# A weight's block sums computed in an earlier stage and passed through DRAM, in a decoder block on one core

## The chip, the core and the metric

The kernel runs on one NeuronCore of a Trainium2 chip. The metric is the time of one execution in microseconds of device time. Several executions give a median. The profile is that of one further execution. It shows five engines: PE (matrix products; PEld loads its weights), DVE (vector), ACT (activations), POOL, and SP, which here only issues DMA transfers. Each engine works through its own list of instructions in order. Transfers issued by SP are one queue, those issued by POOL another, and both move over the core's 16 DMA engines.

## The reference

One decoder block for 1024 tokens of width 1024, all in float32. What matters here, with the attentions left out:

```python
def reference(x, mem, ...):
    h = rmsnorm(x, g_mix_norm[l])
    proj = jnp.einsum('bsd,de->bse', h, w_in[l])
    # q, k, v of two attentions, memory queries, gate logits
    ...
    gates = jax.nn.sigmoid(gate_logit.reshape(b, s, N_BRANCH, D_MODEL))
    merged = gates[:, :, 0] * br_sb + gates[:, :, 1] * br_fox + gates[:, :, 2] * br_mem
    x = x + jnp.einsum('bsd,de->bse', merged, w_out[l])

    h2 = rmsnorm(x, g_mlp_norm[l])
    u = jax.nn.relu(jnp.einsum('bsd,df->bsf', h2, w_ff_up[l]))
    return x + jnp.einsum('bsf,fd->bsd', u * u, w_ff_down[l])
```

`w_out` is 1024x1024, 4 MB.

## The kernel before

**Arithmetic.** A float32 product is made of three passes: each operand is split into a high part (ACT copies it to the matrix engine's type) and a low part (DVE subtracts the high part from the operand), and PE adds high times high, high times low and low times high. The large products are cut into 2x2 blocks of 512 and made with seven block products instead of eight, named P1 to P7, of sums and differences of blocks. For the output projection the right operand is `w_out`, with blocks W11, W12, W21, W22 (the first figure counts the rows). The right sides that aren't a plain block are W12 - W11 (called `wr12` below), `raw2` = W22 - wr12, and the two differences W21 - raw2 and raw2 - W11.

**Stages.** In order of time: norm of the input; projections (to about 500 us); two attentions and the memory attention; three gated branches added up (`merged`, held in tiles `acc`); the output projection with the residual and the second norm (about 957 to 1058 us); the two products of the MLP.

**Output projection.** The order of its products is `OUT = ("P1", "P2", "P6", "P5", "P3", "P7", "P4")`. A product has four tiles of 128 tokens by 512 columns; a tile is 12 matmuls of 128x512 on PE (L2234). `right_side` splits the right operands (`rounded`: a copy on ACT, a subtraction on DVE), `left_side` the left ones. `residual` adds each finished tile to the rows of `x`, which are loaded into tiles `xm` (shown as `h`), on DVE; after a row block's last tile, its square on ACT gives the row sums, `normed` makes the reciprocal root on small tiles (DVE, ACT) and scales the row (half on ACT, L2291; half on DVE, L2293), and `turn_half` transposes it on PE (L2316, four 128x128 pieces at a time) for the MLP. All plain element-wise operations of this part on DVE stand at L1928, the helper `tt`.

**What sets the order.** The program is written as generators that `spawn` starts. An in-kernel planner (`Machine`) runs them against a model of the engines with a cost for each operation (`dve_time`, `act_time`) and a rate for transfers, and issues every instruction in the order in which the model starts it. `spawn(..., late)` sets how urgent a generator is: a larger figure stands back. One run of the planner covers projections, attentions and two branches, a second one the output projection and the first products of the MLP. The third branch, `last_branch`, lies between the two and is ordered in the usual way of the framework. So an instruction added in one place can move others.

**The weight before.** `last_branch` loads the four blocks of `w_out` into the tiles `wr["11"]`, `wr["12"]`, `wr["22"]`, `wr["21"]` (1 MB each, SP). DVE makes wr12 = W12 - W11 there (one 128x2048 subtraction) and at its end `raw2` (four of 128x512). After the split of P6's right operand, `right_side` makes the other two differences in place (eight of 128x512) and then fires `sums_made`, on which `left_side` waits.

In the projections the tiles of the pool `RAW` (`ra` and `rb`, 128x1024) hold weights on their way to sums and splits; `value_steps` and the gate projections store their results to `v_sb` and `gate_scr` through SP.

Of the kernel before, what the change touches and what calls it, by code (L numbers as in the profile page):

```python
# [14 lines left out]
F32 = mybir.dt.float32  # L15
# [3 lines left out]
ALU = mybir.AluOpType  # L19
AX = mybir.AxisListType  # L20

P = 128
# [21 lines left out]
def tile_hybrid_block(  # L44
# [20 lines left out]
    nc = tc.nc  # L65
# [20 lines left out]
    dram = ctx.enter_context(tc.tile_pool(name="dram", bufs=1, space=bass.MemoryType.DRAM))  # L86
# [35 lines left out]
    v_scr = {k: dram.tile([P, ST * 512], F32, name=f"v_{k}", tag=f"v_{k}") for k in ("sb0", "sb1", "fx0", "fx1")}  # L122
    vr_scr = dram.tile([S + 1, 512], F32, name="vr_scr", tag="vr_scr")
    m_scr = [dram.tile([P, 4, 512], F32, name=f"m_scr{c}", tag=f"m_scr{c}") for c in range(2)]
    x2_scr = dram.tile([S, D], F32, name="x2_scr", tag="x2_scr")
    u_scr = dram.tile([P, S // 2], F32, name="u_scr", tag="u_scr")
    s_scr = dram.tile([7 * DFF // 2, S // 2], F32, name="s_scr", tag="s_scr")
# [56 lines left out]
    class Machine:  # L184
# [12 lines left out]
        def spawn(self, gen, late=0.0):  # L197

            done = Event()
            proc = [gen, late, done, None]  # L200
            self.at(self.now, lambda: self.resume(proc, None))
            return done
# [82 lines left out]
    spawn = machine.spawn  # L285
# [7 lines left out]
    def dve_time(*cols):  # L293
        return sum(0.08 + 0.00105 * m for m in cols)

    def transfer(fn, size, issue=0.1, rate=250e3, queue_="SP"):

        yield Op(queue_, issue, fn, 0.0)
        machine.pipe = max(machine.now, machine.pipe) + size / rate
        yield Sleep(machine.pipe + 2.0 - machine.now)  # L300
# [64 lines left out]
    WP, RAW = Places(list(zip(made_w["whi"], made_w["wlo"]))), Places(made_w["raw"])  # L365
# [1002 lines left out]
    prepped, p_ops, landed_ = ({(u, kind): Event() for u in PROJ for kind in KINDS} for _ in range(3))  # L1368
# [160 lines left out]
    def unit_final(u, ct, q, src, of_bank=False):  # L1529
# [29 lines left out]
        else:  # L1559
# [8 lines left out]
                                      t_.rearrange("p (h n) -> p h n", h=2))  # L1568
            yield from counted(u, c, spawn(normed_turned(src, ss, hd, {"mq": gmq, "fxk": gk2, "fxq": gq2}[u], out_), 1.0))

    def masked(t):
        nc.gpsimd.memset(t, 0.0)
        nc.gpsimd.affine_select(out=t[:, 384:], in_=t[:, 384:], pattern=[[-1, P + 1]], compare_op=ALU.is_ge,
                                fill=-NEG, base=0, channel_multiplier=1)
# [10 lines left out]
    def value_steps():  # L1585

        t = yield Get(SN)
        yield Op("DVE", SMALL, lambda: nc.vector.memset(t[0:1, :], 0.0))
        yield from stored(lambda: nc.sync.dma_start(vr_scr[0:1, :], t[0:1, :]), t)
        for c in range(2):  # L1590
            yield in_scr["sbv", c]
            yield Sleep(1.0)
            evs = []
            for g in range(4):
                three = yield Get(SN, 3)

                def issue():
                    for r0, t in zip((1 + g * 256, g * 256), three):
                        nc.sync.dma_start(t.rearrange("p (i n) -> p i n", i=2),
                                          vr_scr[r0:r0 + 256, c * 256:(c + 1) * 256].rearrange("(i p) n -> p i n", p=P))  # L1600
                yield from transfer(issue, P * 4096, 0.2)
                evs.append(spawn(value_step(c, g, *three)))
            for ev in evs:
                yield ev
            machine.fire(stepped[c])
# [239 lines left out]
    with tc.manual_schedule():  # L1845
        spawn(prologue())
        spawn(unit_loads())
        spawn(unit_prep(), -4.0)
        spawn(forget(), 5.0)
        spawn(value_steps(), 0.0)  # L1850
        spawn(second_part())
        spawn(more_banks())
        spawn(load_pairs(), -20.0)
        spawn(memory(), -300.0)
        spawn(after_kv(kv_tasks))
        spawn(all_h([t.done for t in h_tasks]))
        spawn(loader(tasks))
        spawn(operands(), 100.0)
        spawn(units(True))
        spawn(units(False))  # L1860
        spawn(dense(), 3.0)
        machine.run()
        assert all(pair.over.fired for pair in pairs) and "ws" in holder
# [18 lines left out]
    def last_branch(gpool, os_, ws):  # L1882
        b = order[2][0]
        for d2 in range(4):
            w = ws[d2] if d2 < len(ws) else load_w([(0, w_br[b][:, d2 * 256:(d2 + 1) * 256])], 4, 256)
            if d2 == 3:
                hi, lo = right_tiles("P1")
                for q in range(2):
                    raw = wr["11"][:, 2 * q:2 * q + 2]
                    nc.scalar.activation(hi[q], raw, AF.Copy)  # L1890
                    tt(lo[q], raw, f32(hi[q]), ALU.subtract)
            for dd in range(2):
                d = 2 * d2 + dd
                gt = gpool.t("gt", [P, S])
                nc.sync.dma_start(gt, gate_scr[b * D + d * P:b * D + (d + 1) * P, :])
                if d in (1, 2, 3, 4):
                    key = ("11", "12", "22", "21")[d - 1]
                    k_, n_ = int(key[0]) - 1, int(key[1]) - 1
                    nc.sync.dma_start(wr[key], w_out[k_ * 512:(k_ + 1) * 512, n_ * 512:(n_ + 1) * 512].rearrange(
                        "(k p) n -> p k n", p=P))  # L1900
                nc.scalar.activation(gt, gt, AF.Sigmoid)
                if d == 7:
                    nc.scalar.activation(C.t("st", [P, 8])[:, :1], gt[:, :1], AF.Sqrt, bias=one, scale=0.0)
                for half in range(2):
                    cols = slice(half * 512, half * 512 + 512)
                    ps = mmbank()
                    mm3(ps, [((w[0][:, k, dd * P:(dd + 1) * P], w[1][:, k, dd * P:(dd + 1) * P]), os_[k][half])
                             for k in ks])
                    a_, tm = acc[d][:, cols], gpool.t("tmp", [P, 512])
                    tt(tm, ps, gt[:, cols], ALU.mult)  # L1910
                    tt(a_, a_, tm, ALU.add)
                    if half == 0:
                        hi, lo = left["P1" if d < 4 else "P2"][d % 4]
                        nc.scalar.activation(hi, a_, AF.Copy)
                        tt(lo, a_, f32(hi), ALU.subtract)
                if d == 5:
                    tt(wr["12"], wr["12"], wr["11"], ALU.subtract)
                if d >= 4:
                    k = d - 4
                    a11, a21, a22 = acc[k][:, :512], acc[k][:, 512:], acc[d][:, 512:]  # L1920
                    tt(raw1[k], a21, a22, ALU.add)
                    tt(a21, a11, a21, ALU.subtract)
                    tt(a11, raw1[k], a11, ALU.subtract)
        for k in range(4):
            tt(raw2[k], wr["22"][:, k], wr["12"][:, k], ALU.subtract)

    def tt(out_, a_, b_, op):
        nc.vector.tensor_tensor(out_, a_, b_, op)  # L1928
# [10 lines left out]
    wr = {key: RB.t("h", [P, 4, 512]) for key in ("12", "22", "11", "21")}  # L1939
# [18 lines left out]
    for s in range(0, ST, 2):  # L1958
        t = RA.t("h", [P, 2, D])
# [93 lines left out]
    with tc.manual_schedule():  # L2053
# [81 lines left out]
        def rounded(hi, lo, raw, n):  # L2135
            yield Op("ACT", act_time(n), lambda: nc.scalar.activation(hi, raw, AF.Copy))
            yield Op("DVE", dve_time(n), lambda: tt(lo, raw, f32(hi), ALU.subtract))

        def each(late, *gens):
            for ev in [spawn(g, late + 0.2 * i) for i, g in enumerate(gens)]:  # L2140
                yield ev

        def right_side():

            src = {"P2": "21", "P5": "12", "P3": "22", "P7": "11", "P4": "21"}
            for kind in OUT[1:]:
                n = OUT.index(kind)
                if n >= 2:
                    yield out_issued[OUT[n - 2]]
                hi, lo = right_tiles(kind)  # L2150
                if kind == "P6":
                    yield from each(0.0, *(rounded(right[kind][0][k], right[kind][1][k], raw2[k], 512) for k in range(4)))
                else:
                    raw = wr[src[kind]]
                    yield from each(0.0, *(rounded(hi[q], lo[q], raw[:, 2 * q:2 * q + 2], 1024) for q in range(2)))
                machine.fire(right_made[kind])
                if kind == "P6":
                    for key in ("21", "11"):
                        for k in range(4):
                            a_, b_ = (wr[key][:, k], raw2[k])[::1 if key == "21" else -1]  # L2160
                            yield Op("DVE", dve_time(512), lambda: tt(wr[key][:, k], a_, b_, ALU.subtract))
                    machine.fire(sums_made)

        def left_side():
# [570 lines left out]
```

## Time and profile before

| | |
|---|---|
| time, median of 3 runs | 1667.91 us (1666.76 to 1668.11) |
| the profiled execution | 1668.89 us |
| its span | 1667.1 us |
| mean granted PE clock | 0.999 |
| busy: PE, PEld, DVE, ACT, POOL | 1654.5, 1434.6, 1292.5, 848.9, 256.3 us |
| instructions of PE, DVE, ACT, POOL | 9118, 2079, 1474, 440 |
| DMA read and written | 189.83 MB and 92.83 MB |

The span runs from the first to the last instruction of the profiled execution; the time of that execution contains 1.8 us more. A timeline row gives the start in us from the span's beginning, the duration in us, engine, line, operation, result<-operands, the shape and a count; in square brackets stands how long the engine was idle before the row and what it waited for. `SPq` is SP's issue of transfers. A row of windows gives the window, its length, and for PE, PEld, DVE, ACT and POOL the busy time with the number of instructions in it, then the granted PE clock, the busy share of the DMA engines, and GB/s. [...]

### The profile page before, as it was taken

How to read it: one execution, taken by the hardware profiler on the slowest of the kernel's cores; microseconds unless marked ns; L12 is line 12 of the kernel's file. 1: busy time of each engine (PE TensorE's matmuls, PEld its weight loads, DVE VectorE, ACT ScalarE, POOL GpSimd, SP SyncE). 2: the span in 40 equal slices, each digit the busy share in tenths (PEclk: the TensorE clock that was granted, in tenths of full speed). 3: DMA queues.
4: the chain of work that ended last, by engine and by line, in shares of the span. 5: the costliest groups of instructions: out<-in, count | busy, mean ns of one | idle time of the engine just before them, and what ended most of it. 6: DMA issues, size and time to landing. Idle time of an engine off the chain costs nothing.

```text
span 1667.1 us, 24994 instructions
## 1 busy us (share of the span) xinstructions
PE 1654.5 (99%) x9118; PEld 1434.6 (86%) x9118; DVE 1292.5 (78%) x2079; ACT 848.9 (51%) x1474; POOL 256.3 (15%) x440
## 2 busy tenths in 40 slices
PE   9999999999999999999999999999999999999999
PEld 9998899998888888888888887878888888888887
DVE  7978778855459889868878798987777776787875
ACT  6445555535458898877761446533333345333331
POOL 0001000000153142245400011011122120000000
PEclk9999999999999999999999999999999999999999
DMA  7445534468474455577747643144444475564532
GB/s 247 149 161 170 165 114 137 141 182 255 140 237 145 147 160 162 140 222 222 244 142 215 219 168 104 58 158 150 148 158 158 151 275 211 181 213 169 202 126 76
DMA packets 142222, 284.32 MB, mean 171 GB/s; under 512 B 16914, under 2 KB 53330, under 8 KB 142099
## 3 DMA queue, kind: packets, MB, share of 16 engines
q1 hardware_dynamic: 110562, 183.08, 32.5%
q0 software_dynamic: 31536, 99.64, 19.9%
q8 instruction: 72, 1.18, 0.3%
q14 instruction: 52, 0.42, 0.1%
HBM read 189.83 MB, written 92.83 MB: 170 GB/s over the span
## 4 chain that ended last, share of the span: by engine, by line
PE 72%; issue 14%; DVE 7%; POOL 3%; DMA 3%; ACT 1%; SPq 0%; POOLq 0%; ACTq 0%; DVEq 0%
PE pp L1466 11%; PE pp L1154 10%; PE sc L1466 7%; PE pp L2672 7%; PE sc L1154 6%; PE tr L927 4%; PE tr L2672 4%; PE sc L2672 4%; POOL s_scr L2009 3%; PE pv L1466 3%; PE pv L2672 2%; PE sc L944 2%; PE pp L944 2%; DVE h L1928 2%; DVE tmp L1928 1%
## 5 line engine op out<-in xcount | busy, mean ns | idle before, releaser
L1992 PE MATMUL pp<-h,oh 128*128 128x512 f32 x384 | 118.7, 390 | 1.2 <-ACT cu L2077 0.9
L934 DVE TENSOR_TENSOR ptl<-tr,pth 128x512 fp32r<-128x512 f32 (+1 forms) x160 | 99.0, 628 | 23.9 <-ACT pth L932 23.1
L932 ACT ACTIVATE pth<-tr 128x512 fp32r<-128x512 f32 (+1 forms) x160 | 87.4, 557 | 33.5 <-PE sc L944 14.6
L1992 PEld LDWEIGHTS pp<-h,oh 128*128 128x128 f32 x384 | 71.9, 188 | 17.2 <-ACT cu L2077 1.7
L1383 POOL DMA_DIRECT2D raw<-w_in x32 | 24.2, 757 | 394.8 <-DVE la L1065 207.6
L1992 PE MATMUL pp<-h,ol 128*128 128x512 f32 x192 | 74.9, 390 | 0.0
L853 DVE TENSOR_TENSOR_SCAN e<-r,e 128x384 f32<-128x384 f32 (+3 forms) x64 | 66.3, 1044 | 6.8 <-ACT e L838 6.4
L2672 PE MATMUL pp<-h,h 128*128 128x512 f32 x288 | 66.6, 389 | 0.0
L2672 PE MATMUL pp<-sop,sop 128*128 128x512 f32 x288 | 66.6, 389 | 0.0
L2672 PEld LDWEIGHTS pp<-sop,sop 128*128 128x128 f32 x288 | 54.1, 188 | 11.2
L2672 PEld LDWEIGHTS pp<-h,h 128*128 128x128 f32 x288 | 54.1, 188 | 11.2
L927 PE MATMUL tr<-ident,e 128*128 128x128 f32 x416 | 62.5, 272 | 0.0
L927 PEld LDWEIGHTS tr<-ident,e 128*128 128x128 f32 x416 | 50.5, 140 | 9.9 <-DVE ptl L934 0.2
L2009 POOL DMA_DIRECT2D s_scr<-cu x48 | 26.1, 544 | 191.7 <-DVE cu L1999 183.6
L1014 POOL DMA_DIRECT2D h<-sbk_scr x64 | 33.3, 526 | 95.5 <-PE pv L151 29.5
L944 PE MATMUL sc<-pth,v 128*128 128x256 f32 (+1 forms) x170 | 47.4, 301 | 0.0
L2587 ACT ACTIVATE h<-t 128x2048 fp32r<-128x2048 f32 (+1 forms) x9 | 15.4, 1725 | 60.2 <-DVE t L1928 56.1
L1154 PE MATMUL sc<-h,hc 128*128 128x512 f32 (+1 forms) x154 | 44.8, 375 | 0.0
L1928 DVE TENSOR_TENSOR x<-x,pp 128x512 f32<-128x512 f32 x39 | 26.6, 682 | 22.8 <-PE pp L2672 22.8
L1065 DVE TENSOR_TENSOR lb<-raw,hb 128x1024 fp32r<-128x1024 f32 x20 | 24.5, 1223 | 25.6 <-ACT hb L1064 25.5
L2009 POOL DMA_DIRECT2D s_scr<-s x60 | 32.5, 542 | 71.4 <-DVE s L1928 64.8
L1992 PEld LDWEIGHTS pp<-h,ol 128*128 128x128 f32 x192 | 36.0, 188 | 8.1 <-DVE ol L1928 0.6
(792 smaller groups left out, 5540.3 us busy)
## 6 DMA issues: line engine op xcount, KB each, us to landing
ur<-s_scr SPq DMA_DIRECT2D x26, 1024.0 KB
raw<-w_in POOLq DMA_DIRECT2D x32, 512.0 KB, 4.8
raw<-w_up SPq DMA_DIRECT2D x60, 256.0 KB
s_scr<-s POOLq DMA_DIRECT2D x60, 256.0 KB, 2.7
g<-w_down SPq DMA_DIRECT2D x14, 1024.0 KB
s_scr<-cu POOLq DMA_DIRECT2D x48, 256.0 KB, 2.9
h<-sbk_scr POOLq DMA_DIRECT2D x64, 128.0 KB, 3.1
o<-gate_scr SPq DMA_DIRECT2D x32, 256.0 KB
```

The lines of the kernel that those rows point to most:

```text
L853: nc.vector.tensor_tensor_scan(out=back, data0=rho[:, :u][:, ::-1], data1=back, initial=0.0 if last else beta[:, c + u:c + u + 1], op0=ALU ...
L927: nc.tensor.transpose(tr[:, jj * 256 + a * P:jj * 256 + (a + 1) * P], es[a][:, j * P:(j + 1) * P], ident)
L932: yield Op("ACT", act_time(512 - lo_c), lambda: nc.scalar.activation(ph[:, lo_c:], tr[:, lo_c:], AF.Copy))
L934: yield Op("DVE", dve_time(512 - lo_c), lambda: nc.vector.tensor_tensor(pl[:, lo_c:], tr[:, lo_c:], f32(ph[:, lo_c:]), ALU.subtract))
L944: nc.tensor.matmul(pv[0][:, c_:256], pair.v[:, j, b, :], p_[:, jj * 256 + c_:(jj + 1) * 256], start=(k == 0 and n_ == 0 and i == 0), stop= ...
L1014: nc.gpsimd.dma_start(f32(t[k][rows_, :]), src)
L1154: nc.tensor.matmul(ps, a_, b_, start=(first and i == 0), stop=(last and i == n - 1))
L1466: nc.tensor.matmul(out_, a_, b_, start=(first and n == 0 and j == 0), stop=(last and n == 3 and j == len(todo) - 1), skip_group_check=True)
L1928: nc.vector.tensor_tensor(out_, a_, b_, op)
L1992: nc.tensor.matmul(ps, w[a_][:, k * P:(k + 1) * P], h[b_][k], start=(first and k == 0 and i == 0), stop=(last and k == 3 and i == 2), skip ...
L2009: nc.gpsimd.dma_start(s_scr[r0:r0 + P, :], t)
L2672: nc.tensor.matmul(ps, a_[:, c, qs], b_[:, c, :], start=(kind in ("P1", "P2", "P7") and c == 0 and i == 0), stop=(kind in ("P2", "P4", "P3 ...
```

## The change

A new generator `out_sums` makes all four differences in the projections. It starts once the first right operand of one of the gate projections is prepared, and works through `w_out` in four bands of 128 rows per block: take two `RAW` tiles, load four 128x512 pieces (256 KB each, SP), four DVE subtractions, store the four results (256 KB each, SP) to a DRAM tile `wo_scr`, give the tiles back. That is 32 transfers and 16 DVE instructions. A next band's loads into the same tiles come after the stores that read them.

`last_branch` then loads W11, W21 and W22 from `w_out` and the ready difference for `wr["12"]` from DRAM, fetches `raw2` as four transfers after the sixth gate block, and replaces `wr["11"]` by its ready difference with a transfer of 1 MB at its end. `right_side` starts a transfer of 1 MB into `wr["21"]` after P2's split, and P4's split waits for it. The 13 DVE subtractions there are gone.

```diff
+    wo_scr = {key: dram.tile([P, 4, 512], F32, name=f"wo_{key}", tag=f"wo_{key}") for key in ("11", "12", "21", "22")}
...
+    def out_sums():
+
+        yield prepped["ga", "P1"]
+        for k in range(4):
+            got = yield Get(RAW, 2)
+            t11, t12, t21, t22 = (t[:, i * 512:(i + 1) * 512] for t in got for i in range(2))
+
+            def issue():
+                for t, key in ((t11, "11"), (t12, "12"), (t22, "22"), (t21, "21")):
+                    r0, c0 = (int(key[0]) - 1) * 512 + k * P, (int(key[1]) - 1) * 512
+                    nc.sync.dma_start(t, w_out[r0:r0 + P, c0:c0 + 512])
+            yield from transfer(issue, 4 * P * 2048, 0.4)
+            for out_, a_, b_ in ((t12, t12, t11), (t22, t22, t12), (t21, t21, t22), (t11, t22, t11)):
+                yield Op("DVE", dve_time(512), lambda: nc.vector.tensor_tensor(out_, a_, b_, ALU.subtract))
+
+            def store():
+                for t, key in ((t12, "12"), (t22, "22"), (t21, "21"), (t11, "11")):
+                    nc.sync.dma_start(wo_scr[key][:, k, :], t)
+            yield Op("SP", 0.4, store, 3.0)
+            RAW.put(*got)
...
         spawn(value_steps(), 0.0)
+        spawn(out_sums(), 8.0)
...
                 if d in (1, 2, 3, 4):
-                    key = ("11", "12", "22", "21")[d - 1]
+                    key = ("11", "21", "12", "22")[d - 1]
...
-                    nc.sync.dma_start(wr[key], w_out[k_ * 512:(k_ + 1) * 512, n_ * 512:(n_ + 1) * 512].rearrange(
-                        "(k p) n -> p k n", p=P))
+                    nc.sync.dma_start(wr[key], wo_scr["12"] if key == "12" else w_out[
+                        k_ * 512:(k_ + 1) * 512, n_ * 512:(n_ + 1) * 512].rearrange("(k p) n -> p k n", p=P))
...
                 if d == 5:
-                    tt(wr["12"], wr["12"], wr["11"], ALU.subtract)
+                    for k in range(4):
+                        nc.sync.dma_start(raw2[k], wo_scr["22"][:, k, :])
...
-        for k in range(4):
-            tt(raw2[k], wr["22"][:, k], wr["12"][:, k], ALU.subtract)
+        nc.sync.dma_start(wr["11"], wo_scr["11"])
...
                     raw = wr[src[kind]]
+                    if kind == "P4":
+                        yield in21
...
+                if kind == "P2":
+                    in21 = spawn(transfer(lambda: nc.sync.dma_start(wr["21"], wo_scr["21"]), 4 * P * 2048))
                 if kind == "P6":
-                    for key in ("21", "11"):
-                        for k in range(4):
-                            a_, b_ = (wr[key][:, k], raw2[k])[::1 if key == "21" else -1]
-                            yield Op("DVE", dve_time(512), lambda: tt(wr[key][:, k], a_, b_, ALU.subtract))
                     machine.fire(sums_made)
```

The order of instructions changes on DVE and SP in the projections, and on DVE, ACT, SP and PE in the output projection. The rows below give the line, the operation, result<-operands with a number for each buffer, and the shape. Lines of the changed kernel are 1 to 23 higher, and buffer numbers are shifted.

DVE in the projections, from 361.45 to 367.31 us of the profile before; L1396 makes weight sums, L1513 adds product tiles, L1065 splits:

```order
L1396 TENSOR_TENSOR s_155<-raw_153,raw_154 128x1024
L1513 TENSOR_TENSOR sn_149<-sn_149,pv_140 128x512
L1396 TENSOR_TENSOR raw_153<-raw_151,raw_153 128x1024
L1396 TENSOR_TENSOR raw_151<-s_155,raw_151 128x1024
L1513 TENSOR_TENSOR sn_147<-sn_147,pp_135 128x512
L1396 TENSOR_TENSOR raw_152<-raw_152,raw_151 128x1024
L1065 TENSOR_TENSOR la_165<-raw_151,ha_163 128x1024
```

The same stretch with the change; L1585 is `out_sums`:

```order
L1397 TENSOR_TENSOR s_159<-raw_157,raw_158 128x1024
L1514 TENSOR_TENSOR sn_153<-sn_153,pv_144 128x512
L1397 TENSOR_TENSOR raw_157<-raw_155,raw_157 128x1024
L1585 TENSOR_TENSOR ra_168<-ra_168 128x512
L1397 TENSOR_TENSOR raw_155<-s_159,raw_155 128x1024
L1514 TENSOR_TENSOR sn_151<-sn_151,pp_139 128x512
L1397 TENSOR_TENSOR raw_156<-raw_156,raw_155 128x1024
L1585 TENSOR_TENSOR rb_170<-rb_170,ra_168 128x512
L1585 TENSOR_TENSOR rb_170<-rb_170 128x512
L1066 TENSOR_TENSOR la_169<-raw_155,ha_167 128x1024
L1585 TENSOR_TENSOR ra_168<-rb_170,ra_168 128x512
```

Four of the new subtractions stand between the weight's sums and splits that PE waits for.

DVE at the end of the third branch and the start of the output projection, before; `raw_9281` to `raw_9284` are `raw2`, `rb` is the low part of P2's right operand, and the rows on `g_7467` and `raw_9288` make left sums:

```order
L1928 TENSOR_TENSOR lb_9658<-h_9264,hb_9656 128x1024
L1928 TENSOR_TENSOR raw_9288<-g_7467,g_7469 128x512
L1928 TENSOR_TENSOR raw_9281<-h_9262,h_9261 128x512
L1928 TENSOR_TENSOR g_7467<-g_7467 128x512
L1928 TENSOR_TENSOR raw_9282<-h_9262,h_9261 128x512
L1928 TENSOR_TENSOR g_7467<-raw_9288,g_7467 128x512
L1928 TENSOR_TENSOR raw_9283<-h_9262,h_9261 128x512
L1928 TENSOR_TENSOR raw_9284<-h_9262,h_9261 128x512
L1928 TENSOR_TENSOR ol_9664<-g_7466,oh_9660 128x512
L1928 TENSOR_TENSOR rb_9659<-h_9264,ra_9657 128x1024
```

And with the change:

```order
L1951 TENSOR_TENSOR lb_9710<-h_9316,hb_9708 128x1024
L1951 TENSOR_TENSOR raw_9340<-g_7519,g_7521 128x512
L1951 TENSOR_TENSOR ol_9716<-g_7518,oh_9712 128x512
L1951 TENSOR_TENSOR g_7519<-g_7519 128x512
L1951 TENSOR_TENSOR rb_9711<-h_9316,ra_9709 128x1024
L1951 TENSOR_TENSOR g_7519<-raw_9340,g_7519 128x512
L1951 TENSOR_TENSOR h_9684<-h_9684,pp_9700 128x512
```

The four `raw2` rows are gone, one left split (`ol`) stands earlier, and `rb` comes after one left sum fewer.

PE in the output projection where P3 has ended (`pv` is its last tile) and P7 begins (`sc`), before; L2316 are the turns of the rows in `h`:

```order
L2234 MATMUL pv_9655<-ha_9904,ol_9896 128x512
L2234 MATMUL sc_9651<-hb_10013,cu_9931 128x512
L2234 MATMUL sc_9651<-lb_10015,cu_9931 128x512
L2234 MATMUL sc_9651<-hb_10013,cu_9935 128x512
L2316 MATMUL pp_9648<-ident,h_9632 128x128 x4
L2316 MATMUL pp_9649<-ident,h_9632 128x128 x4
L2234 MATMUL sc_9651<-hb_10013,cu_9932 128x512
L2234 MATMUL sc_9651<-lb_10015,cu_9932 128x512
L2234 MATMUL sc_9651<-hb_10013,cu_9936 128x512
L2316 MATMUL pp_9650<-ident,h_9632 128x128 x4
```

And with the change, where L2339 are the turns:

```order
L2257 MATMUL pv_9707<-ha_9970,ol_9889 128x512
L2339 MATMUL pp_9700<-ident,h_9684 128x128 x4
L2339 MATMUL pp_9701<-ident,h_9684 128x128 x4
L2339 MATMUL pp_9702<-ident,h_9684 128x128 x4
L2257 MATMUL sc_9703<-hb_10060,cu_9937 128x512
L2257 MATMUL sc_9703<-lb_10062,cu_9937 128x512
L2257 MATMUL sc_9703<-hb_10060,cu_9941 128x512
```

Three turns stand straight after P3's last matmul, ahead of all of P7; before, three matmuls of P7 stood ahead of the first two turns and three more ahead of the third.

## Prediction

> **What bounds the kernel now.** I read the engine line of the page first, then what the tensor engine (PE) waits for, then its granted clock and its rows around the longest wait, and last the vector engine (DVE) there.
>
> ```profile
> span 1667.1 us, 24994 instructions
> PE 1654.5 (99%) x9118; PEld 1434.6 (86%) x9118; DVE 1292.5 (78%) x2079; ACT 848.9 (51%) x1474; POOL 256.3 (15%) x440
> ```
>
> PE is busy for 1654.5 of 1667.1 us, and its instructions stay as many. So the change can only give back PE's waits and slow stretches, or add some. The waits of PE, in total, times and longest:
>
> ```profile
> PE pp L2316 <- ACT h L2291: 3.0, 1, 3.0
> ...
> PE pp L1992 <- ACT cu L2077: 0.9, 2, 0.7
> ...
> PE sc L2234 <- DVE rb L1928: 0.6, 1, 0.6
> ```
>
> The first and the last lie in the output projection, where the removed work stands. PE there, and DVE's and ScalarE's (ACT's) part of the chain that PE waits for:
>
> ```profile
> 973.68 0.39 PE L2234 MATMUL sc<-ra,cu 128*128 128x512 f32 x1
> 974.63 0.50 PE L2234 MATMUL sc<-rb,cu 128*128 128x512 f32 x1 [0.56 <-DVE rb L1928]
> ...
> 1011.04 0.39 PE L2234 MATMUL pp<-ha,ol 128*128 128x512 f32 x1
> ...
> 1016.49 0.39 PE L2234 MATMUL pv<-ha,ol 128*128 128x512 f32 x1
> 1016.71 0.39 PE L2234 MATMUL sc<-hb,cu 128*128 128x512 f32 x1
> ...
> 1017.16 0.39 PE L2234 MATMUL sc<-hb,cu 128*128 128x512 f32 x1
> 1020.51 1.63 PE L2316 MATMUL pp<-ident,h 128*128 128x128 f32 x8 [2.95 <-ACT h L2291]
> ```
> ```profile
> 1016.37 0.67 DVE L1928 TENSOR_TENSOR h<-h,pp 128x512 f32<-128x512 f32 x1
> ...
> 1019.73 0.72 ACT L2291 ACTIVATE h<-h,st 128x512 f32<-128x512 f32 x1
> ```
>
> A product starts every 0.225 us ((1017.16 - 1016.71) / 2). The one due at 973.68 + 0.23 = 973.91 starts at 974.63: 0.72 lost to DVE's `rb`. The turn (transposes) due at 1017.16 + 0.23 = 1017.39 starts at 1020.51: 3.12 lost. Its chain starts with P3's second sum (1016.37), a tile that PE had ended at 1011.04 + 0.39 = 1011.43: DVE runs five microseconds behind PE. The clock after the wait, with busy time of each engine in a window; the last columns are granted clock, DMA share and GB/s:
>
> ```profile
> 970.00:1010.00 40.00, 39.44 (x174) 32.31 (x174) 40.00 (x59) 20.03 (x35) 8.31 (x4) 1.00 0.32 114
> 1020.50:1021.00 0.50, 0.49 (x4) 0.50 (x5) 0.50 (x1) 0.50 (x1) 0.00 (x0) 0.91 1.11 127
> 1021.00:1024.00 3.00, 3.00 (x14) 2.60 (x12) 2.58 (x5) 3.00 (x7) 0.00 (x0) 0.50 0.92 335
> 1024.00:1024.50 0.50, 0.50 (x4) 0.46 (x3) 0.41 (x1) 0.50 (x3) 0.00 (x0) 0.68 0.15 57
> ```
>
> DVE has no idle time (40.00 of 40) ahead of the wait. After it the clock was half: 0.09 x 0.5 + 0.50 x 3.0 + 0.32 x 0.5 = 1.71 us of PE's time. Without the wait this goes too, as the clock was 1.00 before it. [...] Were the half clock unrelated to the wait, 1.71 would stay, and 1664.4 be the time below.
>
> So 0.72 + 3.12 + 1.71 = **5.55 us** is the most that the change can give here.
>
> **The change part by part.** Removed are 13 DVE instructions.
>
> ```profile
> 932.21 2.28 DVE L1928 TENSOR_TENSOR h<-h,h 128x2048 f32<-128x2048 f32 x1
> ...
> 940.75 1.23 DVE L142 TENSOR_TENSOR lb<-rb,hb 128x1024 fp32r<-128x1024 f32 x1 [1.19 <-ACT hb L141]
> ...
> 971.55 1.29 DVE L1928 TENSOR_TENSOR raw<-h,h 128x512 f32<-128x512 f32 x2
> ...
> 973.36 1.22 DVE L1928 TENSOR_TENSOR rb<-h,ra 128x1024 fp32r<-128x1024 f32 x1
> ...
> 984.71 1.28 DVE L1928 TENSOR_TENSOR h<-raw,h 128x512 f32<-128x512 f32 x2
> ```
>
> One is 2.28 long and far ahead (932.21); I count no gain for it, since DVE waits for ACT behind it (1.19 at 940.75). Four make `raw2` ahead of `rb`, eight the other sums (the last pair at 984.71). Three starts in 973.36 - 971.55 = 1.81 make 0.60 us from one to the next.
>
> (a) `rb` has the four of `raw2` less ahead of it (and by the new order one left sum, which I leave out): it starts 4 x 0.60 = 2.4 earlier, at 970.96, and ends at 972.18, ahead of PE's 973.91: 0.72 comes back. What is late next there: nothing up to 1017.
>
> (b) P3's second sum has 12 x 0.60 = 7.2 us less ahead of it, and one other sum of 0.60 is ordered ahead of it: 1016.37 - 6.6 = 1009.8. PE gives its tile at 1011.43 - 0.72 = 1010.7, so now PE decides. From the sum to the turn the chain takes 1020.51 - 1016.37 = 4.14, so the turn can go at 1014.85. In the new order PE turns straight after P3, at 1016.71 - 0.72 = 1015.99. Margin 1.1: 3.12 and 1.71 come back. The third turn of that row follows on the second scaled half; ACT has one square and one scaling between, both of the scaling's shape (0.72), so 1014.85 + 1.45 = 1016.3 against 1015.99 + 2 x 0.44 = 1016.9 leaves 0.6.
>
> (c) Late next is the turn of the third row block.
>
> ```profile
> 1021.00 0.68 DVE L1928 TENSOR_TENSOR h<-h,pv 128x512 f32<-128x512 f32 x1
> ...
> 1038.98 0.69 DVE L1928 TENSOR_TENSOR h<-h,sc 128x512 f32<-128x512 f32 x1 [1.32 <-PE sc L2234]
> ...
> 1041.70 0.69 DVE L1928 TENSOR_TENSOR h<-h,sc 128x512 f32<-128x512 f32 x1 [2.03 <-PE sc L2234]
> ```
> ```profile
> 1027.22 0.72 ACT L2291 ACTIVATE h<-h,st 128x512 f32<-128x512 f32 x1
> ```
> ```profile
> 1029.46 0.60 PE L2316 MATMUL pp<-ident,h 128*128 128x128 f32 x4
> 1029.81 0.47 PE L2234 MATMUL tr<-hb,cu 128*128 128x512 f32 x1
> 1030.12 0.39 PE L2234 MATMUL tr<-lb,cu 128*128 128x512 f32 x1
> ```
>
> P3's last sum to its scaled row took 1027.94 - 1021.00 = 6.94. PE ends that tile at 1016.88 - 0.72 = 1016.16, so the row is ready at 1023.1, or 1024.9 by DVE's order with no gap closed. PE arrives after four turns of 0.44 (1030.12 - 1029.46 - 0.23) and 30 products: 1015.99 + 1.7 + 6.8 = 1024.5. The new wait is 0 to 0.4, and 1.2 if DVE is slower still; I take 0.3, near the slower walk, since these engines stay full.
>
> (d) Nothing takes the gain back before 1042: DVE itself waits for PE at 1038.98 (1.32) and 1041.70 (2.03), so its later work moves with PE.
>
> (e) Added: 16 subtractions of 0.60 = 9.7 us on DVE, and 32 DMAs of 256 KB (4.2 MB read, 4.2 written) on SP, between rows that stood at 361 to 420 us.
>
> ```profile
> 360.00:440.00 80.00, 80.00 (x374) 67.07 (x373) 47.40 (x62) 36.90 (x60) 7.74 (x11) 1.00 0.70 221
> 380.00:400.00 20.00, 20.00 (x90) 16.57 (x89) 9.09 (x13) 10.85 (x18) 1.50 (x2) 1.00 0.79 246
> 400.00:420.00 20.00, 20.00 (x90) 16.57 (x89) 14.17 (x20) 9.91 (x17) 1.50 (x2) 1.00 0.84 264
> ...
> 960.00:970.00 10.00, 10.00 (x46) 8.29 (x45) 9.97 (x17) 6.05 (x9) 0.00 (x0) 1.00 0.90 334
> ```
> ```profile
> 374.22 0.82 SPq L1253 DMA_DIRECT2D v_sb<-sn  x2
> ```
> ```profile
> 415.48 0.63 ACT L1539 ACTIVATE sn<-sn 128x512 f32<-128x512 f32 x1 [5.12 <-DMA v_sb<-sn]
> 417.73 1.22 DVE L1065 TENSOR_TENSOR la<-s,ha 128x1024 fp32r<-128x1024 f32 x1
> 425.10 0.39 PE L1466 MATMUL sc<-h,la 128*128 128x512 f32 x1
> ```
>
> The subtractions hide in DVE's idle 32.6 of 80 us; with that cover gone each costs up to 0.60, 9.7 in all. SP issues in 0.41 each (0.82 for two): 13 us of a queue that has little else; behind the loads, which wait until the stores of the batch before have read the same tiles out, stand the `v_sb` and gate stores, and ACT waits for such a store already (5.12 at 415.48). The load: 255 GB/s now in 380:420, plus 8.4 MB / 59 us = 142, is 397. If the engines carry 334 / 0.90 = 371, 26 x 40 us = 1.0 MB stay over, 2.8 us late; if with these shorter rows they carry only 264 / 0.84 = 314, 3.3 MB, 10.6 us late. PE uses `la` 425.10 - 418.95 = 6.1 after it is made. Ends: 0 to 10.6 us lost. I take 0, by 2.8 < 6.1: the big transfers resemble 960:970 (334) more.
>
> (f) Added in the output projection: 3 MB more read, of `wr11` (1 MB ahead of `x`), `raw2` and `wr21`.
>
> ```profile
> 959.59 3.61 SPq L1965 DMA_DIRECT2D h<-x  x6
> ```
> ```profile
> 974.49 0.68 DVE L1928 TENSOR_TENSOR h<-h,pp 128x512 f32<-128x512 f32 x1
> ```
>
> One MB at 334 GB/s takes 3.1 us, so `x` comes up to 3.1 later. Its first 512 KB need 1.6 at that rate: landed by 959.6 + 1.6 + 3.1 = 964.3, and first added at 974.49 - 2.4 = 972.1. After that PE makes a tile in 12 x 0.225 = 2.7 while a block needs 1.6. `wr11` is split for P7, which begins at 1016.71, `wr21` for P4 behind it; both are issued about 30 us earlier. `raw2` (1 MB) is issued ahead of `x`, before 959.59, and must have landed by 971: 11 us for 3.1 of transfer. Cost 0 to 1 us, should one of these be late by part of its 3.1; I take 0.
>
> Sum: -5.55 + 0.3 = -5.2 (rounded). The profiled execution took 1668.89, 1.8 outside its span and 0.98 above the median 1667.91. Against itself it gives 1663.7; against the median, **1662.7**.
>
> **The rivals.** (A) is the sum: 1661.9 to 1663.8.
>
> (B) DVE is not moved up by the whole 6.6, as it meets PE in between: were it 3 us late in (b), the turn would wait 3.0 - 1.1 = 1.9 without the clock falling, and the median is 1664.3 (1663.9 to 1666). For it: POOL runs in that stretch too (8.31 of 40). Against: a margin of 1.1.
>
> (C) No gain: the turn, now straight after P3, waits 3 us or more elsewhere and the half clock comes back, or the gain is lost at the `cu` wait. 1667.2 to 1667.9. For it: PE's 3.12 moved, not shortened, is what a chain of reduce and scaling would give; against: (b) and (d).
>
> (D) Slower: stores and loads on SP delay the projections' stores, ACT waits in order, and PE runs out. 10.6 late less the cover of 6.1 is 4.5, without cover 10.6: 1667.2 to 1673.3. It decides (slower than before) from 6.1 + 5.2 = 11.3 us late if all cover counts, 5.2 if none. For it: the 5.12. Against: PE loses nothing in 360:440 today (80.00 of 80). [...]
>
> **How the numbers follow.** A 0.57, B 0.13, C 0.14, D 0.16. A measurement of this kernel tells about 0.2% from no change: 1664.57 and 1671.25. A and most of B are faster (0.66); the rest of B, C and half of D are the same (0.26); the rest of D is slower (0.08). The likeliest is 1662.7. The range runs from 1661.0 (the lowest run, 1666.76, less 5.55, rounded down) to 1668.0, the top of C; D above it and a little more are left out.
>
> **What would show it.** Right: no PE wait over 1 us in the output projection, clock 1.00 at 1021 to 1024, `rb` made before PE asks; 360:440 with PE at 80.00. Wrong: a turn's wait of 2 us or more, a clock of 0.50 anywhere new, or PE waits in the projections on `ha`, `la` or `h`, behind an ACT wait on `v_sb` or `gate_scr`.

## The result and the profile after

The changed kernel takes 1676.16 us (median of 6 runs, 1675.9 to 1676.85) against 1668.03 (6 runs): slower, at a ratio of 1.0047 (95% interval 1.0036 to 1.0058). Forecast were 1662.7 and a range to 1668.0. The profiled execution took 1675.98, its span 1674.2, 7.1 more than before.

The engine line of the page:

```profile
span 1674.2 us, 25068 instructions
...
PE 1656.9 (99%) x9118; PEld 1434.9 (86%) x9118; DVE 1293.7 (77%) x2082; ACT 847.9 (51%) x1474; POOL 255.6 (15%) x440
```

What PE waited for, in total, times and longest:

```profile
PE sc L1467 <- ACT sn L1506: 6.1, 2, 3.4
...
PE sc L1467 <- DVE lb L1066: 1.0, 1, 1.0
PE pp L2015 <- ACT cu L2100: 0.9, 2, 0.7
```

The two waits of the output projection (`pp` on `h`, `sc` on `rb`) are gone from this list; new ones, on `sn` and `lb`, stand in the projections. To compare the runs I use one figure below, PE's loss: the time from each matmul's start to the next one's, less the usual step for that shape, added up over a stretch. It holds the waits and the time lost to a slower clock.

| PE's loss, us | before | changed |
|---|---|---|
| projections, 340 to 480 | 0 | 12.1 |
| output projection, 950 to 1060 | 5.9 | 0.3 |

That is +12.1 - 5.6 = 6.5 of the 7.1 by which the span grew. The forecast gain is there in full, and a loss of twice its size lies in front of it.

**The output projection**, changed kernel. Rows of PE and ACT at the first turn, and a window of 40 us ahead of it:

```profile
1027.92 0.39 PE L2257 MATMUL pv<-ha,ol 128*128 128x512 f32 x1
1028.15 1.47 PE L2339 MATMUL pp<-ident,h 128*128 128x128 f32 x12
1029.38 0.47 PE L2257 MATMUL sc<-hb,cu 128*128 128x512 f32 x1
```
```profile
1025.75 0.73 ACT L2314 ACTIVATE h<-h,st 128x512 f32<-128x512 f32 x1 [0.88 <-DVE st L388]
...
1026.99 0.71 ACT L2314 ACTIVATE h<-h,st 128x512 f32<-128x512 f32 x1
```
```profile
982.00:1022.00 40.00, 40.00 (x178) 33.13 (x177) 37.91 (x54) 21.12 (x37) 7.92 (x4) 1.00 0.40 149
```

The first scaled row is ready at 1026.48 and PE turns it at 1028.15: a margin of 1.7 (forecast 1.1). The second scaled row is ready at 1027.70, and its turn is reached about 0.9 after 1028.15: a margin of 1.3 (forecast 0.6). DVE now idles 2.1 of these 40 us, where it idled 0.1 in the kernel before, and the clock stays at 1.00 (so too from 1020 to 1060).

**The projections**, changed kernel. SP's queue at the second band of `out_sums` (L1589 stores it, L1582 loads the next), then the waits of SP and of ACT from 340 to 480 us, and ACT's and PE's rows behind them:

```profile
388.55 0.33 SPq L1589 DMA_DIRECT2D wo<-ra  x1
389.28 1.44 SPq L1589 DMA_DIRECT2D wo<-rb  x2
390.81 0.42 SPq L1589 DMA_DIRECT2D wo<-ra  x1
396.77 0.81 SPq L1582 DMA_DIRECT2D ra<-w_out  x2
397.67 0.86 SPq L1582 DMA_DIRECT2D rb<-w_out  x2
398.58 0.90 SPq L1254 DMA_DIRECT2D v_sb<-sn  x2
```
```profile
SPq L1582 <- DMA wo<-ra: 14.4, 3, 5.5
```
```profile
ACT sn L1540 <- DMA v_sb<-sn: 15.1, 2, 8.1
...
ACT L1540 <- DMA v_sb<-sn: 4.9, 1, 4.9
```
```profile
404.32 0.63 ACT L1540 ACTIVATE sn<-sn 128x512 f32<-128x512 f32 x1 [8.09 <-DMA v_sb<-sn]
...
428.83 1.32 ACT L1540 ACTIVATE sn<-sn 128x512 f32<-128x512 f32 x2 [7.04 <-DMA v_sb<-sn]
430.06 0.58 ACT L1506 ACTIVATE sn<-sc 128x512 f32<-128x512 f32 x1
```
```profile
426.86 0.39 PE L1467 MATMUL pp<-h,lc 128*128 128x512 f32 x1
430.69 1.22 PE L1467 MATMUL sc<-h,ha 128*128 128x512 f32 x2 [3.44 <-ACT sn L1506]
...
443.23 0.73 PE L1467 MATMUL sc<-g,hb 128*128 128x512 f32 x2 [2.64 <-ACT sn L1506]
```

Read it as a chain. SP has issued the last store by 391.2. The next entry of its queue is a load into the same tile; it goes out at 396.8, once the stores have landed (their data has arrived), and SP issues nothing in those 5.5 us. Behind it stands the third pair of `v_sb` stores, which goes out at 398.58; in the kernel before, the third pair went out here:

```profile
385.32 0.81 SPq L1253 DMA_DIRECT2D v_sb<-sn  x2
```

Not all of these 13 us are SP's wait of the second band: DVE finished the pair only at 393.0, as ACT had already waited 4.9 us behind the first band's wait. From there to 398.58 are 5.6 us.

ACT needs a tile that these stores read, and waits 8.09 us, with everything behind it on ACT. The next time it is 7.04, and the copy of a PSUM bank that PE needs (`sn<-sc`, 430.06) is among what stands behind, so that PE waits 3.44. PE's wait of 2.64 at 443.23 hangs on the same chain by another way:

```profile
433.06 1.37 SPq L1621 DMA_DIRECT2D sn<-vr_scr  x2
```
```profile
440.30 0.69 DVE L1602 TENSOR_TENSOR sn<-sn,sn 128x512 f32<-128x512 f32 x1 [3.79 <-DMA sn<-vr_scr]
```
```profile
441.03 0.72 ACT L1244 ACTIVATE sn<-sn 128x256 fp32r<-128x256 f32 x2 [3.85 <-DVE sn L1602]
...
442.61 0.57 ACT L1506 ACTIVATE sn<-sc 128x512 f32<-128x512 f32 x1
```

In SP's queue this load stands behind a gate store, which needs ACT's result of 428.83, and behind the four stores of the last band. So it goes out late, DVE waits for it, ACT for DVE, and PE for ACT.

### The profile page after: what moved, and what is told of

Read it like the earlier page. It is cut to its first block, busy times and chain, and to the rows that moved or that the text cites. A ratio compares the mean times of both kernels' runs of the same rounds, so it can differ in the third digit from the quotient of the medians.

```text
span 1674.2 us, 25068 instructions
## 1 busy us (share of the span) xinstructions
PE 1656.9 (99%) x9118; PEld 1434.9 (86%) x9118; DVE 1293.7 (77%) x2082; ACT 847.9 (51%) x1474; POOL 255.6 (15%) x440
## 4 chain that ended last, share of the span: by engine, by line
PE 79%; issue 6%; DVE 5%; DMA 4%; POOL 1%; ACT 1%; SPq 0%; POOLq 0%; ACTq 0%; DVEq 0%
PE pp L1467 10%; PE pp L2695 7%; PE sc L1467 6%; PE sc L1155 5%; PE pp L2015 5%; PE pv L1155 5%; PE pp L1155 4%; PE tr L2695 4%; PE sc L2695 4%; PE tr L928 4%; PE sc L2015 3%; PE pv L1467 3%; PE pv L2695 2%; PE sc L945 2%; PE pp L2257 2%
## 5 line engine op out<-in xcount | busy, mean ns | idle before, releaser
L838 ACT ACTIVATE r<-pp 128x384 f32<-128x384 f32 (+3 forms) x96 | 48.0, 500 | 12.6 <-DVE pp L845 8.2
```

Of the source, the lines that this page charges most:

```text
L838: nc.scalar.activation(rho[:, :u], sc[:, :u], AF.Sigmoid, scale=HD ** -0.5)
```

## The experiments

**Theory W**: a wait in SP's order (a load waits for the landing of the stores ahead of it, and stores of other work stand behind it). **Theory B**: the added bytes on the DMA engines. B is the term by which the prediction had priced this part.

**1. Stores landed before the next loads.** The edit:

```diff
-            yield Op("SP", 0.4, store, 3.0)
+            yield from transfer(store, 4 * P * 2048, 0.4)
             RAW.put(*got)
```

> The changed kernel with one line of out_sums different: the planner takes the four stores of a band as a transfer that has to land (size and 2 us) before the tiles are given back, so the next band's loads are issued later, behind stores of other work, instead of straight behind the stores whose landing they wait for. Same transfers, same bytes, same arithmetic. Theory W (a wait in SP's order: the loads wait 4 to 5.5 us for those stores to land, and the v_sb and gate stores behind them come late): ACT's waits for v_sb fall from 20.0 to about 5 us, PE's loss in 380 to 460 us falls from 12.1 to under 2, time 1663 to 1667. Theory B (bytes: 8.4 MB more on the 16 engines): the loss stays at 9 to 12, time 1673 to 1677.

Measured: 1663.64 us (10 runs), ratio 0.9972 (0.9963 to 0.9982) to the kernel before. PE's loss in 340 to 480 is 0, as W had it. SP's and ACT's waits for these stores, and three windows (the last three columns: clock, DMA share, GB/s):

```profile
SPq L1582 <- DMA wo<-ra: 2.0, 2, 1.9
```
```profile
ACT L1540 <- DMA v_sb<-sn: 2.8, 1, 2.8
ACT sn L1540 <- DMA v_sb<-sn: 2.4, 1, 2.4
```
```profile
380.00:400.00 20.00, 20.00 (x90) 16.57 (x89) 11.23 (x17) 12.08 (x19) 1.50 (x2) 1.00 1.01 335
400.00:420.00 20.00, 20.00 (x90) 16.57 (x89) 15.64 (x21) 8.23 (x14) 1.50 (x2) 1.00 0.93 310
420.00:440.00 20.00, 20.00 (x90) 16.53 (x90) 13.25 (x19) 10.05 (x17) 3.24 (x5) 1.00 1.02 343
```

The same windows of the changed kernel:

```profile
380.00:400.00 20.00, 19.41 (x85) 15.38 (x84) 9.24 (x13) 9.12 (x14) 1.50 (x2) 1.00 0.88 280
400.00:420.00 20.00, 19.00 (x84) 15.44 (x83) 14.71 (x20) 7.61 (x13) 1.50 (x2) 1.00 0.81 266
420.00:440.00 20.00, 16.56 (x67) 13.22 (x67) 9.57 (x15) 7.75 (x13) 3.24 (x5) 0.91 1.00 327
```

The kernel without loss moves more bytes per us in each window. B, taken as a lack of capacity, falls. The room in the changed kernel lay behind SP's wait and not in it: while SP waited (391.2 to 396.8) the DMA engines were full, and then ACT stood still.

```profile
391.20:396.80 5.60, 5.01 (x21) 3.45 (x21) 3.95 (x6) 3.82 (x7) 0.75 (x1) 1.00 0.97 305
396.80:404.30 7.50, 7.50 (x35) 6.21 (x34) 0.86 (x2) 0.00 (x0) 0.00 (x0) 1.00 0.74 258
```

The edit moves other instructions of this stretch too, on PE, DVE, ACT and SP, so this run alone doesn't show that the loads' place is what matters.

**2. The added part alone**: the kernel before with `out_sums`, unread.

> The kernel before plus out_sums as the change has it; its results in DRAM are not read, and the output projection makes its sums as before. This prices the added part alone. If the gain in the output projection is 5.6 and the loss in the projections 12.1, and the two don't touch: 1668.0 + 12.1 = 1680.1 (1678.5 to 1681.5). Were a part of the loss due to the fetches later on, it would be nearer to 1676.

Measured: 1682.35 us (4 runs), ratio 1.0084 (1.0067 to 1.0101): 13.9 above the 1668.43 of the kernel before in that comparison. PE's loss is 13.8 in 340 to 480 and 5.9 in the output projection. The loss belongs to the added part alone, and the two parts add up. The forecast's 1680.1 was 2 too low, and its range ended at 1681.5; this execution lost 1.6 more in the projections than the changed kernel did.

**3. The waits nearly without bytes**: as 2, with 16 of 512 columns.

```diff
-                    nc.sync.dma_start(t, w_out[r0:r0 + P, c0:c0 + 512])
+                    nc.sync.dma_start(t[:, :16], w_out[r0:r0 + P, c0:c0 + 16])
...
-                    nc.sync.dma_start(wo_scr[key][:, k, :], t)
+                    nc.sync.dma_start(wo_scr[key][:, k, :16], t[:, :16])
```

> The kernel before plus out_sums whose 32 transfers carry 16 columns instead of 512 (8 KB each, 0.26 MB in all) and whose subtractions are as narrow; order and waits as in the added part, results unread. Theory W: the loads still wait for the landing of the stores in front of them, some 2 to 4 us each instead of 4 to 5.5, so a part of the loss stays, 3 to 9 us: 1671 to 1677. Theory B: no bytes, no loss: 1667 to 1669.

Measured: 1668.71 us, ratio 1.0001 (0.9992 to 1.0011); no loss in 340 to 480. This missed W's figure: the waits are there, but short.

```profile
SPq L1582 <- DMA wo<-ra: 5.9, 3, 3.2
```

Up to 500 us every engine has the same order of instructions here, in experiments 2 and 6, and in the changed kernel. So the order that the planner made costs nothing by itself. The subtractions are as narrow as the transfers here; at full width they are free in experiments 1 and 4, in other orders.

**4. The bytes without the waits**: the kernel before with an `out_sums` that loads all bands twice, subtracts and stores nothing.

```diff
-        for k in range(4):
+        for k in (0, 1, 2, 3, 0, 1, 2, 3):
...
-            yield Op("SP", 0.4, store, 3.0)
             RAW.put(*got)
```

> The kernel before plus an out_sums that loads the four bands of the weight twice (32 loads of 256 KB, 8.4 MB, the bytes of the added part, all read) with the subtractions after each band (32 instead of 16), and stores nothing; results unread. No load waits for a store to land, only for DVE. Theory W: loss under 2 us, 1667 to 1670. Theory B: the loss of the added part, 9 to 12: 1677 to 1680.

Measured: 1668.63 us, ratio 1.0002 (0.9992 to 1.0011); no loss in 340 to 480, with twice the added subtractions on DVE. The bytes, here all read, and DVE's work cost nothing there; experiment 1 has the written bytes too, without loss. So 3 and 4 together: neither the wait in the order nor the bytes cost anything alone. The loss needs a long wait, and the wait is long where the stores are big (SP's longest is 3.2 us in experiment 3 with 8 KB a store, and 5.2 with 256 KB in experiment 2, in the same order of instructions). In this sense bytes do matter: through the time to the landing.

**5. An earlier place**: `prepped["fxk", "P1"]` instead of `prepped["ga", "P1"]`, nothing else.

> The changed kernel with out_sums begun two stages of the projections earlier (at the forgetting attention's key projection, near 220 us, where the transfers of the kernel before move 45 to 165 GB/s instead of 206 to 264), and nothing else: the next band's loads still follow the stores on SP with two other stores between at most. If the harm is the wait times the slow landing of stores in a loaded stretch: SP's waits for those stores fall below 6 us in all, ACT waits for no store, no loss of PE in 200 to 340 or 340 to 480 us, time 1662 to 1665. If the wait in SP's order harms by itself wherever it stands: a loss of 5 us or more stays, 1668 or more.

Measured: 1663.84 us (8 runs), ratio 0.9972 (0.9962 to 0.9983); no loss in 200 to 340 nor in 340 to 480.

```profile
SPq L1582 <- DMA wo<-ra: 4.9, 2, 2.5
```

ACT still waits once for a `v_sb` store, 5.3 us long, as the kernel before did (5.1); "ACT waits for no store" was said too strongly. The change as written is as fast as with the line of experiment 1 if it only stands where the transfers are few (45 to 165 GB/s from 220 to 300 us of the kernel before, 246 and 264 in the two windows from 380 to 420). This edit too moves other instructions.

**6. Half the width**: as 3, with 256 columns.

> The kernel before plus out_sums with 256 of 512 columns (128 KB a transfer, 4.2 MB in all), results unread: the dose between 8 KB (no loss, SP's waits for stores 5.9 us) and 256 KB (loss 13.8, waits 14.6). If PE has a fixed cover of some 5 to 6 us for each late store, the loss is far below half of 13.8, 0 to 4 us: 1668 to 1672. If loss goes with bytes, 7: 1675.

Measured: 1669.08 us, ratio 1.0004 (0.9994 to 1.0013); loss 0.03. SP's and ACT's waits:

```profile
SPq L1582 <- DMA wo<-ra: 9.8, 3, 4.9
```
```profile
ACT sn L1540 <- DMA v_sb<-sn: 8.6, 3, 5.4
ACT L1540 <- DMA v_sb<-sn: 2.9, 1, 2.9
```

The dose is not linear: SP's waits of 5.9 and 9.8 us in all cost nothing, 14.4 cost 12.1. ACT's longest wait here, 5.4, costs PE nothing. But there is no fixed cover beyond which everything is loss: in the changed kernel PE lost about 1.1 us after ACT's wait of 4.9, 1.3 after that of 8.1, and after that of 7.0 it waited 3.44 at once. The waits follow each other there, and that each one used up slack which the next lacked fits the order, but wasn't tried alone.

**9. The other tile.** Eight half bands take turns in the two tiles, so that the loads still come soon after the stores but write the other tile:

```diff
-            t11, t12, t21, t22 = (t[:, i * 512:(i + 1) * 512] for t in got for i in range(2))
+            t11, t12, t21, t22 = (got[j % 2][:, i * 256:(i + 1) * 256] for i in range(4))
```

> The changed kernel with out_sums working in eight half bands of 256 columns that take turns in the two tiles: the next loads still stand straight behind the stores on SP, but write the other tile, so they wait for stores of two half bands earlier, which landed long before. Same 8.4 MB, twice as many transfers (64 of 128 KB), planner's landing not changed. Theory W: SP's waits of loads for stores under 2 us in all (14.4 in the changed kernel), no loss of PE in 340 to 480 us, 1662 to 1665. If it is the loads' place straight behind the stores, or bytes with writes, the loss stays: 1670 or more.

Measured: 1666.1 us (10 runs), ratio 0.9986 (0.9975 to 0.9997); loss 2.1 in 340 to 480, one wait of 1.94 at 396.71. In SP's list the loads (L1583) wait for no `wo` store; the one wait of this kind belongs to a store (L1590):

```profile
SPq L1590 <- DMA wo<-ra: 1.1, 1, 1.1
```

Ten of the 12.1 are gone. Of six batches of loads from 370 to 443 us two go out straight behind stores of the half band before (370.20, 432.80); ahead of the others stand one to four transfers of other work. The batches are half as large too, and in experiment 6, with stores of 128 KB, SP's longest wait was 4.9 us, against 5.2 with 256 KB in experiment 2. So this run doesn't show the tile's part alone. W's "no loss" was too much. The 1.94 hang on a load of other work, which SP issued at 386.06 without a wait and for which DVE waited until 393.26. So this rest may be a cost of the bytes; it was not tried.

**7 and 8. What in the output projection gives the gain.** Both start from experiment 1. In 7, DVE makes `raw2` again; in 8, the other eight differences.

```diff
 7:
-                    for k in range(4):
-                        nc.sync.dma_start(raw2[k], wo_scr["22"][:, k, :])
...
+        for k in range(4):
+            tt(raw2[k], wr["22"][:, k], wr["12"][:, k], ALU.subtract)
 8:
-        nc.sync.dma_start(wr["11"], wo_scr["11"])
...
+                    for key in ("21", "11"):
+                        for k in range(4):
+                            a_, b_ = (wr[key][:, k], raw2[k])[::1 if key == "21" else -1]
+                            yield Op("DVE", dve_time(512), lambda: tt(wr[key][:, k], a_, b_, ALU.subtract))
```

> The first experiment's kernel (stores landed before the next loads) with raw2 made by DVE at the end of the third branch again, four subtractions, and not fetched. By the working of the prediction: the wait at rb (0.72) comes back, the turn doesn't wait (its input at 1016.3 against 1016.7): 1663.6 + 0.7 = 1664.3, PE's loss in the output projection 0.42 + 0.7 = 1.1. If those four decide the turn too, 3 us or more: 1667.

> The first experiment's kernel with the other two block sums made by DVE after P6's split again, eight subtractions, and not fetched; raw2 is fetched. By the working of the prediction: no wait at rb; P3's second sum at 1016.37 - 2.4 = 1014.0, the turn ready at 1018.1 against PE at 1016.7: a wait of 1.4, clock unbroken, 1663.6 + 1.4 = 1665.0, PE's loss in the output projection 1.8. If any wait there halves the clock for a window, 1.7 more: 1666.7.

Measured: 7 takes 1662.5 us (4 runs), ratio 0.9961 (0.9947 to 0.9976), PE's loss in the output projection 0.4; 8 takes 1663.72 us (7 runs), ratio 0.9970 (0.9960 to 0.9981), loss 0.95. Forecast were losses of 1.1 and 1.8. In 7 `rb` is ready although the four subtractions stand ahead of it; in 8 the turn waits 0.2, not 1.4:

```profile
969.72 1.22 DVE L1950 TENSOR_TENSOR rb<-h,ra 128x1024 fp32r<-128x1024 f32 x1
```
```profile
972.92 0.39 PE L2256 MATMUL sc<-rb,cu 128*128 128x512 f32 x1
```
```profile
1018.53 1.09 PE L2338 MATMUL pp<-ident,h 128*128 128x128 f32 x8 [0.20 <-ACT h L2313]
```

In 7 PE uses `rb` at 972.92, which is 1.0 earlier than it was due before (973.91), and DVE starts it at 969.72, which is 3.6 earlier. Of these 3.6 none is due to `raw2`, and the whole stretch is 1.0 earlier, so DVE stands 2.6 better from what is left out further ahead. The 13th subtraction, wr12 (2.28), fits, though it wasn't taken away alone; the prediction had counted nothing for it. Not all 13 are needed: taking away 9 leaves the same loss as taking away all in experiment 1 (0.4), and taking away 5 leaves about 0.5 more.

## Why the prediction was wrong

- **(a), (b): right in direction and size.** 5.55 less 0.3 was forecast; PE's loss fell from 5.9 to 0.3. The half clock went with the wait (1.00 from 1020 to 1060 of the changed kernel), so the 1.71 belonged to it; but the same wait need not bring it (experiments 4 and 6, last section), so these 1.71 us were not a sure part of the gain.
- **(a), a term mis-sized**: wr12's 2.28 was set to nothing because DVE waited for ACT behind it (1.19). Experiment 7 leaves 2.6 us for which nothing else of this size stands there. A wait of 1.19 could hide at most 1.19 of it. Experiment 8 points the same way: the turn waits 0.2 where the prediction's sum gave 1.4. wr12 alone wasn't tried.
- **(c)**: 0.3 was set for a new wait of the third row block's turn; no wait for a turn is left in the list of the changed kernel, and the loss of 0.3 in the table consists of steps of 0.1. **(d)** holds: what came back by 1060 stayed.
- **(e) is the step that failed**: "0 to 10.6 us lost. I take 0". It cost 12.1. It was priced by a backlog of bytes over an assumed capacity of 371 or 314 GB/s, and experiments 1 and 4 move as many bytes without loss. The text beside it has the right chain, "the loads, which wait until the stores of the batch before have read the same tiles out", with the `v_sb` stores behind them and ACT behind those, but the wait had no price of its own. Three such waits measured 14.4 us; ACT waited 4.9, 8.1 and 7.0 us behind them, where the kernel before had 0.7 and 5.1; and after two of PE's waits its clock was half as well (0.50, last section). The cover of 6.1, taken from one row of `la`, isn't a figure that holds for each wait: 5.4 cost nothing in experiment 6, 4.9 was followed by a loss of 1.1 here. The subtractions were priced at 0 as long as DVE has idle time. They cost nothing in experiment 4, but here two of them (412.92, 414.65) stand ahead of the `lb` for which PE waits 1.00.
- **The rival (D)** had the mechanism, 0.16, and a top of 1673.3; the time went beyond it by 2.9, and the clock's loss (3.4 below) and the recurring of the wait with each band were not counted in it. The sign named for it, PE waits in the projections behind an ACT wait on `v_sb`, is what the trace shows.
- **(f) holds**: in experiment 1 all the fetches are there and the output projection loses 0.4.

## What to carry to other kernels

Here a load that had to wait for stores to land held up what stood behind it in its queue: SP issued nothing for 5.5 us. Ask of each added load what its target tile is read by, how long that reader's landing takes in this stretch, and which stores with a waiting engine stand behind it. A change that adds work in one stage and saves in another is best priced as two kernels. Here one line, by which the planner gives the tiles back only after the landing, turned 8 us lost into 4.8 gained.

## What the runs showed of the hardware

After a PE wait of 2.64 us the clock was half (0.50 from 444.06 to 447.47). The windows around it and around the wait of 3.44 (granted clock in the third column from the end):

```profile
430.00:434.00 4.00, 3.31 (x8) 2.64 (x9) 2.39 (x3) 3.54 (x7) 0.75 (x1) 0.57 1.04 398
...
443.00:448.00 5.00, 4.77 (x14) 3.78 (x15) 1.55 (x2) 1.65 (x4) 0.00 (x0) 0.66 0.72 266
```

They lose 0.43 x 4 + 0.34 x 5 = 3.4 us of PE's time. Waits of 1.00 (at 416.53) and 1.94 (experiment 9) left the clock alone: it is 1.00 from 414 to 420 of the changed kernel and from 396 to 404 of experiment 9. The length doesn't decide alone, though. In experiment 4 the turn waits as long as in the kernel before (2.95 there), and the clock stays at 1.00:

```profile
1020.38 1.09 PE L2335 MATMUL pp<-ident,h 128*128 128x128 f32 x8 [2.97 <-ACT h L2310]
```
```profile
1021.00:1024.00 3.00, 3.00 (x19) 2.50 (x18) 2.49 (x5) 3.00 (x7) 0.00 (x0) 1.00 0.86 322
```

Experiment 6 shows the same (a wait of 2.96, clock 1.00); in experiment 2 the wait is 3.0 and PE's loss in the output projection 5.9, as in the kernel before with its half clock. What decides stays open.

The stretches at half clock were equally long: 0.50 from 1020.91 to 1024.32 in the kernel before, from 430.41 to 433.82 and from 444.06 to 447.47 in the changed one, each 3.41 us long, with 1.00 in the windows behind them (1024.32 to 1030, 433.83 to 444.06, 447.48 to 460).

Stores of 256 KB in a stretch where the DMA engines were full (share 0.97) took 5.5 us from the last issue to the landing that SP waited for; in experiment 3 the same 32 transfers with 8 KB each held SP for 3.2 at most.
